# Low parts of streamed weights in a two-layer hybrid backbone: subtraction on VectorE, or negation and an adding transfer

## Chip, cores and metric

The kernel runs on one core of one Trainium2 chip. The metric is the device time of one execution in microseconds (us), lower is better. The engines are called PE (TensorE; PEld is its weight load), DVE (VectorE), ACT (ScalarE), POOL (GpSimd) and SP (SyncE, which issues most transfers).

## The reference

Two layers of a backbone over 256 latent tokens and 256 context tokens of width 1024, in float32. The large products with weights are what matters here:

```python
u = rms_norm(h, norm1_g[l]) * (1.0 + sc1) + sh1
a_x, a_g, b_q, b_f, b_i, b_o, c_qkv, m_g = split_projection(u @ w_in[l])
...
h = h + gt1 * merge_branches(ya, yb, yc, m_g, w_branch[l], w_out[l])
h = h + gt2 * sq_relu_ffn(rms_norm(h, norm2_g[l]) * (1.0 + sc2) + sh2, ffn_w1[l], ffn_w2[l])
```

Between them stand three mixers (a gated linear recurrence in chunks, a neighbourhood attention, a bidirectional RG-LRU). Layer 0 computes both token streams (512 columns), the second half of layer 1 only the latent stream (256 columns).

## The kernel before

All large weights stand in HBM as 296 pieces of 128 x 1024 float32 (512 KB), 148 for each layer, in the order of use. A product in float32 accuracy is made of three products in fp32r: with weight = hi + lo and activation = xhi + xlo, it adds hi·xhi, hi·xlo and lo·xhi. So each piece needs two tiles: `whi`, the rounded weight, and `wlo`, what rounding left.

`arriving` (L209) has SP load a piece into a `raw` tile (3 buffers). `weights` (L214) takes a `wlo` and a `whi` tile (4 buffers each) and calls `split` (L224): ACT casts `raw` to `whi` (L226), and DVE subtracts, `wlo = raw - whi` (L227). `mm3` (L233) then issues for each of 8 blocks of 128 rows the three products (L240, L241, L242), 24 matmuls for a piece; `mm3_pairs` (L246, products L253 to L255) does two pieces at a time, and `tok` (L1013, products L1027 to L1029) and `down_pieces` have groups that use four pieces at once.

The main loop (the end of `hybrid_kernel`) works piece by piece. `fetch(n)` calls `weights` until n pieces are ready; before a piece's products are issued three more are fetched (one more ahead of a group of four). With four buffers, the `wlo` and `whi` tiles that the piece three places ahead is to use are those that the piece just ended leaves. Between the runs of products `lanes.tick()` issues steps of the mixers' chains, on all engines. A scheduler at build time sets the order on each engine from this program.

The first four pieces (`tok` of the first head) come with a `raw` tile of their own from `start()`, and one of them is subtracted on POOL. POOL else has little: scaling of `gf`, the rotary tables `ctab` (`rope_tables`, L318), and 15 transfers: the attention's bias tables (`bias`, L960) and the LRU's weights (`gw`, L968). A transfer into a buffer waits in its queue until that buffer is free, and what stands behind it in the same queue waits too. SP's queue has the `raw` pieces and, from the second third of layer 0 on, 72 transfers of 512 KB for the modulation (`arow`, L343) and 8 of `araw`.

Of the kernel before, what the change touches and what calls it, by code (L numbers as in the profile page):

```python
# [10 lines left out]
F32 = mybir.dt.float32  # L11
# [5 lines left out]
ALU = mybir.AluOpType  # L17
# [9 lines left out]
NPIECE = 148  # L27
# [29 lines left out]
def merge_order(l):  # L57
    # some gates first, while the mixers' chains end
    count = {}
    for part in MERGE[l].split():  # L60
        bi = int(part[0])
        for what in part[1:]:
            i = count.get((bi, what), 0)
            count[bi, what] = i + 1
            yield bi, BRANCH_ORDER[bi], {"g": "gate", "p": "proj"}[what], i
# [35 lines left out]
class Piece:  # L101
    """Products with streamed weights: body(weights) yields after each run of products."""
# [5 lines left out]
class Lanes:  # L108
    """Chains of dependent steps that are issued between the runs of products.

    A step yields the time that the vector engine needs for what it issued, and how many runs more the chain waits."""
# [43 lines left out]
def hybrid_kernel(  # L155
# [58 lines left out]
    def weights(l, key, raw=None, eng=nc.vector):  # L214
        cols = {"tok": 4 * P, "proj": 2 * P}.get(key[0], P)
        raw = arriving(l, key) if raw is None else raw
        lo = wpool.tile([P, 1024], F32R, tag="wlo", name="wlo", bufs=4)
        hi = wpool.tile([P, 1024], F32R, tag="whi", name="whi", bufs=4)
        split(hi, lo, raw, eng=eng)
        v = lambda t: t.rearrange("p (k c) -> p k c", c=cols)  # L220
        return v(hi), v(lo)

    def split(hi, lo, src, scale=None, eng=nc.vector):
        # hi <- rounded part of scale * src, lo <- the rest  # L224
        if scale is None:
            nc.scalar.copy(hi, src)  # L226
            eng.tensor_tensor(out=lo, in0=src, in1=hi.bitcast(F32), op=ALU.subtract)  # L227
        else:
            nc.scalar.mul(hi, src, scale)
            nc.vector.scalar_tensor_tensor(  # L230
                out=lo, in0=src, scalar=scale, in1=hi.bitcast(F32), op0=ALU.mult, op1=ALU.subtract
            )
# [13 lines left out]
    def mm3_pairs(dsts, ws, x, nk, c0, c1):  # L246
        # two pieces at a time, so that x may still be arriving
        for i in range(0, len(dsts), 2):
            for k in range(nk):
                xhi, xlo = (t[:, c0:c1] for t in x(k))  # L250
                for p_, (whi, wlo) in zip(dsts[i:i + 2], ws[i:i + 2]):
                    d = p_[:, c0:c1]
                    nc.tensor.matmul(d, lhsT=whi[:, k, :], rhs=xhi, start=(k == 0), stop=False)  # L253
                    nc.tensor.matmul(d, lhsT=whi[:, k, :], rhs=xlo, start=False, stop=False)
                    nc.tensor.matmul(d, lhsT=wlo[:, k, :], rhs=xhi, start=False, stop=(k == nk - 1))  # L255
                if k % 2:
                    yield
# [5 lines left out]
    def layer_scalars():  # L263
# [13 lines left out]
        for l in range(DEPTH):  # L277
            # f = lb + (1 - lb) * (1 + tanh) / 2 as offset and slope
            lb = cpool.tile([P, 2, 2, 4], F32, name=f"lb{l}")
            if l == 0:  # L280
                nc.vector.tensor_copy(cum, e[:, :, 0, :])
            else:
                nc.vector.tensor_add(cum, cum, e[:, :, l, :])
            nc.vector.tensor_sub(lb[:, 0], cum, e[:, :, 0, :])
            nc.vector.tensor_scalar(out=lb[:, 1], in0=lb[:, 0], scalar1=-0.5, scalar2=0.5, op0=ALU.mult, op1=ALU.add)
            nc.vector.tensor_scalar(out=lb[:, 0], in0=lb[:, 0], scalar1=0.5, scalar2=0.5, op0=ALU.mult, op1=ALU.add)
            lbs.append(lb)
# [31 lines left out]
    def rope_tables(l):  # L319
        # ctab[:, cos|sin, tile, k|q, head, :], with the norm's gains and the scores' scale  # L320
        for sc in range(2):
            for i, qk in enumerate((1, 0)):
                g = gf[l][:, 2 * sc + qk, :]
                for hd in range(2):
                    for tt in range(2):
                        nc.gpsimd.tensor_tensor(out=ctab[:, sc, tt, i, hd, :], in0=cst[:, sc, tt, :], in1=g, op=ALU.mult)

# [1 line left out]
    mod = [cpool.tile([P, 3, 2, 16], F32, name=f"mod{l}") for l in range(DEPTH)]  # L329

    def modulation_rows():
        # most sections, a row for each feature: the vector engine has time while the tensor engine is busy
# [34 lines left out]
    def last_modulation():  # L367
        # the last section: four groups of columns in four parts of the array
# [55 lines left out]
    def column_sums(parts, n, tag="A"):  # L424
        # sums over the features, one column for each 128 tokens
        p_ = psum(tag, "nss")
        for c in range(n):
            for i, t in enumerate(parts):
                nc.tensor.matmul(
                    p_[:, c:c + 1], lhsT=t[:, c * P:(c + 1) * P], rhs=ones, start=(i == 0), stop=(i == len(parts) - 1)  # L430
                )
        return p_
# [5 lines left out]
    def spread(r, n, tag="A"):  # L438
        # a row of n * 128 columns in every partition
# [14 lines left out]
    def modulated(u, r, a, b, k, s):  # L454
        # u = h * r * a + b in high and low parts
# [29 lines left out]
    def small_rstd(ss, n, temps):  # L485
        # 1 / sqrt(ss / n + eps) for a few columns: a first guess from the exponent, two steps
# [6 lines left out]
        # with x = v * r * r: r * (15 - 10 x + 3 x^2) / 8, but for the factor 3 / 8, then r * (3 - x) / 2 with that factor  # L493
# [14 lines left out]
    def first_half():  # L508
        # the latent stream's norm, before its products are issued
# [5 lines left out]
    def hgrn(l, j, TF, Q, vtok, sog, ys):  # L515
# [4 lines left out]
        # products over blocks, states of the context stream  # L520
# [9 lines left out]
        # within blocks of 64 tokens, the blocks of a tile side by side  # L530
# [7 lines left out]
        def place(b, src, shift):  # L538
            # blocks in the upper (b = 0) or the lower half of the partitions
# [13 lines left out]
        def mixed(t, hh, c0, n):  # L553
            # [first halves of slot 0 | second halves of slot 1] of the 2*hh blocks in columns c0..c0+n
# [17 lines left out]
        # A^T[s, t] of both directions, level by level  # L572
        Tt = TF[:]
        width = T2
        for lev in range(8):
# [11 lines left out]
            # widen the products to blocks of 2*hh  # L587
# [30 lines left out]
        # final states of the context stream  # L618
# [18 lines left out]
        # outputs, token-major  # L637
# [34 lines left out]
    def attention(l, j, qk, vtok, bias, ys):  # L672
        Tq = T2 if l == 0 else TL
        misc = two_k("misc")
        # normalised keys and queries, token-major: [k | q] of two heads for each 128 tokens
# [23 lines left out]
        # rotary embedding of the latent tokens  # L699
# [48 lines left out]
        def softmax(qt, sc):  # L748
            # both heads at once
# [55 lines left out]
        def applied(qt):  # L805
            # both heads at once, in two parts of the array
# [87 lines left out]
    def fin_query(Tq, Q, p_):  # L894
        # twice the silu
# [5 lines left out]
    def fin_outgate(l, Tq, sog, p_):  # L901
        # the gain over four times (1 + tanh)
# [17 lines left out]
    def fin_gelu(Tq, ge, p_):  # L920
        # twice the tanh GeLU
# [12 lines left out]
    def mixer_pieces(l):  # L934
        T = T2 if l == 0 else TL
        heads = []
        for j in range(4):
# [9 lines left out]
            def opened(nm, m=m, j=j):  # L947
                # tiles of a chain, when its first piece begins
# [9 lines left out]
                if nm == "tok":  # L958
                    m.bias = four_k("bias", (4, TL))
                    (nc.gpsimd if l or j else nc.sync).dma_start(out=m.bias, in_=biasd[l, j])  # L960
                    # [v of both mixers | k and q], two blocks of tokens each
# [4 lines left out]
                if nm in ("ax", "ag") and not hasattr(m, "gw"):  # L966
                    m.gw = two_k("gw").rearrange("p (a b) -> p a b", b=P)
                    nc.gpsimd.dma_start(out=m.gw, in_=lruw[l, j])  # L968
# [21 lines left out]
            def group(ws, m=m, opened=opened, closed=closed):  # L990
                # the first products, while the modulation arrives
# [70 lines left out]
    def merge_pieces(l):  # L1062
# [7 lines left out]
        def gate_tile(bi, d):  # L1070
            # several gates in a tile
# [78 lines left out]
    def down_pieces(l, kind, sub, x, section, T, finished, after, pre=None):  # L1150
        # pieces d = 0..7 into the residual; with after, the last four by streams, so that a norm can start early
# [119 lines left out]
    def start():  # L1271
# [51 lines left out]
        def busy(n):  # L1323
            # keeps the tensor engine's clock up while the first data arrive
# [30 lines left out]
        def arrive():  # L1355
            # what the products of the first chunk need
# [11 lines left out]
        def later():  # L1368
            # what the products of the first chunks don't need
# [11 lines left out]
        def ahead(k, n):  # L1381
            # within the products of chunk k, what those of chunk k + 2 need
# [24 lines left out]
    # weights run ahead of the pieces that use them  # L1407
# [154 lines left out]
```

## Time and profile before

| what | us |
|---|---|
| two timed runs | 1528.32 and 1531.29 |
| their median | 1529.8 |
| span of the profiled execution, first to last instruction | 1526.3 |

The profile is of one execution. Its span leaves out what lies around the first and the last instruction; the median of the timed runs is 3.5 us above it, and that is taken as what lies around.

### The profile page before, as it was taken

The numbers are of one execution on the slowest core, as the hardware profiler recorded it, in microseconds if no ns is written. First come the engines' busy times: TensorE is split into PE (matmuls) and PEld (weight loads), VectorE is DVE, ScalarE is ACT, GpSimd is POOL, SyncE is SP. The second block draws the span as 40 slices with busy tenths as digits, with TensorE's granted clock in tenths as the row PEclk, the third lists the DMA queues.
The fourth block names the chain that finished last, engine by engine and source line by source line (L and its number), as shares of the span: only waits on it lengthen the run. The fifth ranks groups of instructions, "written<-read, shape, count | busy, mean of one in ns | idle before, by whom it ended". The sixth has DMA issues, their size and how long they took to land.

```text
span 1526.3 us, 24145 instructions
## 1 busy us (share of the span) xinstructions
PE 1513.7 (99%) x9554; PEld 1300.8 (85%) x9554; DVE 1115.9 (73%) x2118; ACT 735.0 (48%) x1229; POOL 26.4 (2%) x57
## 2 busy tenths in 40 slices
PE   9999999999999999999999999999999999999999
PEld 4778788878888889888888889888888899999999
DVE  6776768586478898988685856778787856776664
ACT  3457575666333333532322323475766854454442
POOL 0200000020000000000000000000000000000000
PEclk9999999999999999999999999999999999999999
DMA  9413122221273562445463532313313345755553
GB/s 368 146 53 104 56 90 70 70 77 62 91 250 136 187 240 70 171 174 206 139 220 127 204 126 82 133 63 126 104 70 105 109 167 182 274 167 184 186 183 125
DMA packets 61793, 217.36 MB, mean 142 GB/s; under 512 B 7792, under 2 KB 9456, under 8 KB 61680
## 3 DMA queue, kind: packets, MB, share of 16 engines
q1 hardware_dynamic: 59328, 209.88, 39.5%
q0 software_dynamic: 1648, 5.77, 1.2%
q8 instruction: 75, 1.23, 0.3%
q14 instruction: 38, 0.31, 0.1%
q10 hardware_dynamic: 704, 0.17, 0.1%
HBM read 214.74 MB, written 1.05 MB: 141 GB/s over the span
## 4 chain that ended last, share of the span: by engine, by line
PE 96%; DVE 2%; ACT 1%; issue 1%; DMA 0%; SPq 0%; DVEq 0%
PE pd L240 7%; PE pd L242 7%; PE pd L241 7%; PE pf L242 5%; PE pf L240 5%; PE pf L241 5%; PE pg L240 5%; PE pg L241 4%; PE pg L242 4%; PE ptok L1027 3%; PE ptok L1029 3%; PE ptok L1028 3%; PE lv L547 2%; PE pp L241 2%; PE pp L240 2%; PE pp L242 2%
## 5 line engine op out<-in xcount | busy, mean ns | idle before, releaser
L226 ACT CAST whi<-raw 128x1024 fp32r<-128x1024 f32 x296 | 310.3, 1050 | 477.0 <-PE pd L241 157.2
L227 DVE TENSOR_TENSOR wlo<-raw,whi 128x1024 fp32r<-128x1024 f32 x295 | 360.3, 1223 | 151.2 <-ACT whi L226 149.4
L242 PE MATMUL pd<-hhi,wlo 128*128 128x256 f32 (+1 forms) x544 | 177.8, 327 | 0.0
L240 PE MATMUL pd<-hhi,whi 128*128 128x256 f32 (+1 forms) x544 | 177.8, 327 | 0.0
L241 PE MATMUL pd<-hlo,whi 128*128 128x256 f32 (+1 forms) x544 | 177.7, 327 | 0.0
L354 DVE CUSTOM_DVE_ANT_0 junk<-arow,crow 128x1024 bf16<-128x1024 f32 x144 | 173.3, 1219 | 2.2 <-DMA arow<-in_adaw 2.0
L241 PE MATMUL pf<-xlo,whi 128*128 128x256 f32 (+1 forms) x464 | 155.0, 334 | 0.0
L242 PE MATMUL pf<-xhi,wlo 128*128 128x256 f32 (+1 forms) x464 | 155.0, 334 | 0.0
L240 PE MATMUL pf<-xhi,whi 128*128 128x256 f32 (+1 forms) x464 | 155.0, 334 | 0.0
L240 PE MATMUL pg<-xhi,whi 128*128 128x512 f32 (+1 forms) x384 | 131.5, 342 | 0.0
L241 PE MATMUL pg<-xlo,whi 128*128 128x512 f32 (+1 forms) x384 | 129.2, 336 | 0.0
L242 PE MATMUL pg<-xhi,wlo 128*128 128x512 f32 (+1 forms) x384 | 129.2, 336 | 0.0
L1145 DVE SCALAR_TENSOR_TENSOR h<-pd,mod,h 128x256 f32<-128x256 f32 x120 | 54.9, 480 | 81.2 <-PE pd L242 79.2
L241 PEld LDWEIGHTS pd<-hlo,whi 128*128 128x128 f32 x544 | 103.5, 190 | 8.8
L240 PEld LDWEIGHTS pd<-hhi,whi 128*128 128x128 f32 x544 | 103.5, 190 | 8.8
L242 PEld LDWEIGHTS pd<-hhi,wlo 128*128 128x128 f32 x544 | 103.5, 190 | 8.6
L241 PEld LDWEIGHTS pf<-xlo,whi 128*128 128x128 f32 x464 | 88.1, 190 | 8.8
L242 PEld LDWEIGHTS pf<-xhi,wlo 128*128 128x128 f32 x464 | 88.1, 190 | 8.7
L240 PEld LDWEIGHTS pf<-xhi,whi 128*128 128x128 f32 x464 | 88.0, 190 | 8.7
L1027 PE MATMUL ptok<-whi,xhi 128*128 128x512 f32 (+1 forms) x224 | 87.4, 395 | 1.1 <-DVE h L1145 1.1
L1029 PE MATMUL ptok<-wlo,xhi 128*128 128x512 f32 (+1 forms) x224 | 84.4, 377 | 0.0
L1028 PE MATMUL ptok<-whi,xlo 128*128 128x512 f32 (+1 forms) x224 | 84.2, 376 | 0.2 <-DVE xlo L463 0.2
(329 smaller groups left out, 3240.0 us busy)
## 6 DMA issues: line engine op xcount, KB each, us to landing
raw<-in_wpack SPq DMA_DIRECT2D x296, 512.0 KB, 3.5
arow<-in_adaw SPq DMA_DIRECT2D x72, 512.0 KB, 4.7
a<-in_ada0w SPq DMA_DIRECT2D x16, 512.0 KB, 10.4
araw<-in_lastw SPq DMA_DIRECT2D x8, 512.0 KB, 6.3
bias<-in_biasd POOLq DMA_DIRECT2D x7, 512.0 KB, 4.3
h<-in_xT SPq DMA_DIRECT2D x4, 512.0 KB, 5.5
gw<-in_lruw POOLq DMA_DIRECT2D x8, 256.0 KB, 2.9
out<-h SPq DMA_DIRECT2D x8, 128.0 KB, 2.0
```

What stands on the lines that cost most here:

```text
L226: nc.scalar.copy(hi, src)
L227: eng.tensor_tensor(out=lo, in0=src, in1=hi.bitcast(F32), op=ALU.subtract)
L240: nc.tensor.matmul(d, lhsT=whi[:, k, :], rhs=xhi, start=(k == 0), stop=False)
L241: nc.tensor.matmul(d, lhsT=whi[:, k, :], rhs=xlo, start=False, stop=False)
L242: nc.tensor.matmul(d, lhsT=wlo[:, k, :], rhs=xhi, start=False, stop=(k == nk - 1))
L354: nc.vector.tensor_tensor_reduce(out=junk, in0=raw, in1=crow[s], scale=1.0, scalar=0.0, op0=ALU.mult, op1=ALU.add, accum_out=section_of(l, ...
L547: nc.tensor.matmul(dst, lhsT=lhs(b), rhs=rhs(b), start=True, stop=True)
L1027: nc.tensor.matmul(dst, lhsT=xhi[:, k, tsl], rhs=whi[:, kk, :], start=(k == 0), stop=False)
L1028: nc.tensor.matmul(dst, lhsT=xlo[:, k, tsl], rhs=whi[:, kk, :], start=False, stop=False)
L1029: nc.tensor.matmul(dst, lhsT=xhi[:, k, tsl], rhs=wlo[:, kk, :], start=False, stop=(k == KD - 1))
L1145: nc.vector.scalar_tensor_tensor(out=h[:, d, sl], in0=p_[:, sl], scalar=mods(l, section, s)[:, d:d + 1], in1=h[:, d, sl], op0=ALU.mult, op ...
```

## The change

Except for the first four pieces, `wlo` is no longer subtracted. ACT makes `whi` from `raw` as before. DVE writes `wlo = -whi`, with one input. POOL then issues a transfer from HBM that reads the raw piece a second time and adds it to what stands in `wlo`. DVE's step no longer reads `raw`. The `bias` and `gw` transfers, which stood on POOL's queue, go to SP's.

```diff
     def weights(l, key, raw=None, eng=nc.vector):
         cols = {"tok": 4 * P, "proj": 2 * P}.get(key[0], P)
-        raw = arriving(l, key) if raw is None else raw
         lo = wpool.tile([P, 1024], F32R, tag="wlo", name="wlo", bufs=4)
         hi = wpool.tile([P, 1024], F32R, tag="whi", name="whi", bufs=4)
-        split(hi, lo, raw, eng=eng)
+        if raw is not None:
+            split(hi, lo, raw, eng=eng)
+        else:
+
+            nc.scalar.copy(hi, arriving(l, key))
+            nc.vector.tensor_scalar_mul(lo, hi.bitcast(F32), -1.0)
+            nc.gpsimd.dma_start(out=lo, in_=wpack[l * NPIECE + PIECE[key]], accum_op=ALU.add)
...
-                    (nc.gpsimd if l or j else nc.sync).dma_start(out=m.bias, in_=biasd[l, j])
+                    nc.sync.dma_start(out=m.bias, in_=biasd[l, j])
...
-                    nc.gpsimd.dma_start(out=m.gw, in_=lruw[l, j])
+                    nc.sync.dma_start(out=m.gw, in_=lruw[l, j])
```

On POOL the program before has, from the start of layer 0 on, this order (`gf` and `ctab` are the gains and the rotary tables, `msk` the masks of the recurrence, `gw` and `bias` the transfers named above; the numbers count buffers):

```order
L1375 TENSOR_SCALAR gf1_74<-gf1_74 128x64 x2
L326 TENSOR_TENSOR ctab_75<-cst_72,gf0_73 128x64 x8
L1379 CAST msk_76<-mskf_397 128x384
L968 DMA gw_808<-in_lruw 128x512
L960 DMA bias_1063<-in_biasd 128x1024
L968 DMA gw_1564<-in_lruw 128x512
L960 DMA bias_1814<-in_biasd 128x1024
L968 DMA gw_2329<-in_lruw 128x512
L960 DMA bias_2569<-in_biasd 128x1024
L326 TENSOR_TENSOR ctab_75<-cst_72,gf1_74 128x64 x16
L968 DMA gw_3094<-in_lruw 128x512
```

The changed program has there, and from there to its end:

```order
L1380 TENSOR_SCALAR gf_74<-gf_74 128x64 x2
L331 TENSOR_TENSOR ctab<-cst,gf_73 128x64 x8
L1384 CAST msk<-mskf 128x384
L224 DMA wlo<-in_wpack 128x1024 x36
L331 TENSOR_TENSOR ctab<-cst,gf_74 128x64 x16
L224 DMA wlo<-in_wpack 128x1024 x256
```

The 15 transfers are gone and 292 adding ones stand in their place, with the second set of tables between the 36th and the 37th.

On SP the program before has, from the last loads of the setup on (`raw` are the weight pieces, `mskf` the masks, `arow` the modulation's rows):

```order
L1376 DMA idh<-in_consts 128x64
L1378 DMA mskf<-in_masks 128x384
L211 DMA raw<-in_wpack 128x1024 x2
L960 DMA bias<-in_biasd 128x1024
L211 DMA raw<-in_wpack 128x1024 x53
```

The changed program has there:

```order
L211 DMA raw<-in_wpack 128x1024 x2
L965 DMA bias<-in_biasd 128x1024
L211 DMA raw<-in_wpack 128x1024 x8
L973 DMA gw<-in_lruw 128x512
L211 DMA raw<-in_wpack 128x1024 x2
L965 DMA bias<-in_biasd 128x1024
L211 DMA raw<-in_wpack 128x1024 x7
L973 DMA gw<-in_lruw 128x512
```

The transfers of `gw` and `bias` now stand between those of the pieces; the later ones stand in layer 1 in the same way.

## Rows read from the trace of the kernel before

**Rows 1.** Page, parts 1 and 2: busy us of each engine; TensorE's granted clock in 40 slices.
```profile
PE 1513.7 (99%) x9554; PEld 1300.8 (85%) x9554; DVE 1115.9 (73%) x2118; ACT 735.0 (48%) x1229; POOL 26.4 (2%) x57
...
PEclk9999999999999999999999999999999999999999
```

**Rows 2.** Page, part 4: the chain that ended last, by engine.
```profile
PE 96%; DVE 2%; ACT 1%; issue 1%; DMA 0%; SPq 0%; DVEq 0%
```

**Rows 3.** Windows: stretch, length, busy us (instructions) by engine, PEclk, DMA share, GB/s.
```profile
550.00:690.00 140.00, 138.38 (x795) 122.06 (x794) 122.78 (x223) 56.84 (x90) 0.00 (x0) 1.00 0.46 165
690.00:880.00 190.00, 190.00 (x840) 157.34 (x839) 145.43 (x229) 55.32 (x68) 0.00 (x0) 1.00 0.51 177
1188.00:1245.00 57.00, 57.00 (x482) 53.49 (x481) 40.46 (x84) 39.33 (x71) 0.00 (x0) 1.00 0.39 132
1245.00:1305.00 60.00, 60.00 (x502) 60.00 (x502) 42.45 (x69) 29.68 (x49) 0.00 (x0) 1.00 0.54 183
1305.00:1350.00 45.00, 43.55 (x391) 41.05 (x391) 33.50 (x70) 22.02 (x37) 0.00 (x0) 1.00 0.64 232
1350.00:1500.00 150.00, 150.00 (x1253) 150.00 (x1252) 97.35 (x140) 72.58 (x114) 0.00 (x0) 1.00 0.57 187
```

**Rows 4.** Timeline, layer 1's MLP: start, us, instruction [idle before it <- releaser].
```profile
1399.04 1.05 ACT L226 CAST whi<-raw 128x1024 fp32r<-128x1024 f32 x1 [1.79 <-PE pd L241]
...
1400.12 1.23 DVE L227 TENSOR_TENSOR wlo<-raw,whi 128x1024 fp32r<-128x1024 f32 x1 [0.47 <-ACT whi L226]
...
1407.84 0.28 PE L242 MATMUL pf<-xhi,wlo 128*128 128x256 f32 x1
```

**Rows 5.** Windows, only instructions on raw: DVE, ACT, POOL busy us (count), PEclk, DMA.
```profile
550.00:690.00 140.00, 30.47 (x25) 26.26 (x25) 0.00 (x0) 1.00 0.46 165
690.00:880.00 190.00, 42.87 (x35) 36.87 (x35) 0.00 (x0) 1.00 0.51 177
1188.00:1245.00 57.00, 17.03 (x14) 15.18 (x15) 0.00 (x0) 1.00 0.39 132
1245.00:1305.00 60.00, 25.71 (x21) 21.52 (x22) 0.00 (x0) 1.00 0.54 183
1305.00:1350.00 45.00, 14.92 (x13) 13.30 (x13) 0.00 (x0) 1.00 0.64 232
1350.00:1500.00 150.00, 64.68 (x53) 54.55 (x53) 0.00 (x0) 1.00 0.57 187
```

**Rows 6.** Groups by form, DVE: operation, shapes, count | busy us, mean ns | idle before.
```profile
L227 DVE TENSOR_TENSOR wlo<-raw,whi 128x1024 fp32r<-128x1024 f32 x295 | 360.3, 1223 | 151.2 <-ACT whi L226 149.4
L560 DVE COPY km<-KK 128x512 f32<-128x512 f32 x24 | 10.6, 440 | 1.9 <-PE lv L547 1.5 <-PE tp L793 0.3
L560 DVE COPY km<-KK 128x256 f32<-128x256 f32 x24 | 7.0, 293 | 0.6 <-PE tp L793 0.5
```

**Rows 7.** Tile bias: POOL's transfers of 512 KB, ns min/median/max; and time to landing.
```profile
L960 POOL DMA_DIRECT2D bias<-in_biasd x7: 536/536/542, 45.3 to 1097.6; - x7
...
DMA to landing us min/median/max: 3.6/5.3/7.5
```

**Rows 8.** DMA queues from 0 to 38 us: GB/s in 40 equal slices.
```profile
GB/s 0 6 183 356 343 350 393 379 376 423 384 302 418 414 405 410 414 427 418 418 423 418 414 440 397 410 414 414 435 418 418 414 427 414 427 377 373 336 344 230
```

**Rows 9.** Timeline, a `wlo` of a group's end and its first use: two of seven places.
```profile
604.52 1.22 DVE L227 TENSOR_TENSOR wlo<-raw,whi 128x1024 fp32r<-128x1024 f32 x1
...
605.94 0.40 PE L255 MATMUL pf<-xhi,wlo 128*128 128x256 f32 x2
...
1151.27 1.22 DVE L227 TENSOR_TENSOR wlo<-raw,whi 128x1024 fp32r<-128x1024 f32 x1
...
1156.81 0.40 PE L242 MATMUL pff<-xhi,wlo 128*128 128x512 f32 x1
```

**Rows 10.** Timeline of SP and of POOL as layer 1 nears: transfers.
```profile
880.01 0.33 SPq L211 DMA_DIRECT2D raw<-in_wpack  x1
...
881.77 0.54 POOL L960 DMA_DIRECT2D bias<-in_biasd  x1 [564.48 <-DVE mod L354]
```

## The prediction

> **What bounds the kernel now.** I read the page's busy times first, then the chain that ended last, then windows by stage, then the timeline of one piece, and last the transfers. PE is busy 1513.7 us, 99% of the span [rows 1], and 96% of the chain is PE [rows 2]; its granted clock is full all along [rows 1]. So an engine beside PE can save nothing but PE's idle time, 1526.3 - 1513.7 = 12.6 us. DVE, which the change relieves, is at 73% [rows 1] and stands for 2% of the chain [rows 2].
>
> The windows show that the stages differ in what lies behind PE [rows 3]. From 1245 us on (layer 1's merge and MLP, 256 columns) PE runs 1253 matmuls in 150 us; at 24 to a piece that is 52 pieces, one each 2.87 us, with the DMA engines at 0.57. From 690 to 880 us (layer 0's MLP, 512 columns) 840 matmuls take 190 us, 5.43 us a piece, with a DMA share of 0.51. The same weights are thus consumed almost twice as fast at the end.
>
> The timeline of one piece shows the slack [rows 4]. ACT starts a cast at 1399.04 when PE lets go of the buffer (1.79 us of idle before it, ended by PE), DVE has the low part ready at 1400.12 + 1.23 = 1401.35, and PE first reads it three pieces later, at 1407.84. So 6.5 us are free there.
>
> **The change, part by part.** *DVE.* 292 subtractions of 1223 ns go and 292 negations come, an operation with one input that no row has in this size. The nearest are copies: 293 ns for 256 columns and 440 ns for 512 [rows 6], which is 147 ns for 256 more, so 440 + 2 x 147 = 734 ns for 1024. From below I bound it by the 440 ns of half the size, from above by the subtraction's 1223; I take 0.73, as it continues a row of the nearest kind. DVE loses 292 x (1.22 - 0.73) = 143 us of work. What lies on the path is at most the 12.6 us above, and I take 0: PE does not wait for DVE in the long stages, whose windows are full.
>
> *The moved transfers.* `gw` and `bias` go from POOL's queue to SP's, where one that waits would hold up the pieces behind it. In the trace only one buffer came free late against its place on SP: at 881.77 us, while SP issued the next piece at 880.01 [rows 10]. A slip of 1.8 us stands before three loaded `raw` buffers; 0. POOL's tables now stand between two adding transfers, in layer 0, where the slack is larger than in rows 4; 0.
>
> *The adding transfers, as work of the DMA engines.* This is the term that decides. No row shows one. Each must bring 512 KB from HBM, fetch the 512 KB that stand in `wlo`, and write 512 KB. The nearest row is a plain transfer when the engines are saturated: 410 to 427 GB/s for most of the first 38 us [rows 8], so 524 KB / 420 GB/s = 1.25 us. Call the DMA engines' time for one adding transfer A. From below it is 1.25 us (the fetch and the addition are free, as if it were a plain one); less than a plain one, or a gain, I exclude, as the piece is still loaded once more. From above I take 4 us, some three plain ones: two reads, and a write that does not overlap them. I take two reads at the saturated rate, A = 2.5, since two sources go in for each result.
>
> A stage lasts at least as long as its DMA engines have work: share times length [rows 3] plus A for each piece, counted by ACT's casts [rows 5].
>
> - 690 to 880: 0.51 x 190 + 35 x 2.5 = 184 of 190 us, hidden; 550 to 690: 64 + 25 x 2.5 = 127 of 140, hidden.
> - 1188 to 1245: 22.2 + 15 x 2.5 = 59.7, +2.7.
> - 1245 to 1305: 32.4 + 22 x 2.5 = 87.4, +27.4.
> - 1305 to 1350: 28.8 + 13 x 2.5 = 61.3, +16.3.
> - 1350 to 1500: 85.5 + 53 x 2.5 = 218, +68.
>
> Together +114 us. Ahead of 550 us the pieces come more slowly and nothing is added.
>
> Here a rule of the Trainium skill can be weighed. What the rows have is only the plain rate [rows 8]. "Collectives: The Full Stack", in the section on the bandwidth ceiling, says of reductions done by the DMA engines that the addition itself is free and that the cost is the two source reads in the same ring, which halves the rate (measured there as a ratio of 1.93). By that rule A is 1.93 x 1.25 = 2.4 us (an estimate with that page's ratio) and the sum of the four stages +104. No row here shows it.
>
> *The adding transfers, as a longer chain.* After ACT's cast the old chain had 1.22 us; the new one has 0.73 on DVE, POOL's issue, and the landing. POOL's plain transfers of this size landed 3.6 to 7.5 us after issue, median 5.3 [rows 7]; with 1.25 for the second read I take 6.5. The chain becomes 0.73 + 6.5 - 1.22 = 6.0 us longer. In layer 0's long stretches and in rows 4 (6.5 us) that is covered. It is not covered where a group of four pieces ends and the next buffers come free late: seven places, of which the first leaves 605.94 - 605.74 = 0.2 us and the last 1156.81 - 1152.49 = 4.3 us [rows 9]; over the seven the mean is 3.0. So 7 x (6.0 - 3.0) = +21 us. What is queued behind POOL's wait for a negation is only further adding transfers; what is queued behind PE's wait is everything.
>
> A second rule speaks against the change: "SBUF — State Buffer", under who interferes with whom, says that a `tensor_scalar` in a two-port mode locks GpSimd out of the port by which it writes its descriptors. POOL's issue took 536 ns [rows 7], so each issue could start at most one negation later; by the rule the chain would be up to 0.73 us longer, 7 x 0.73 = 5 us in the sum above, and no row here has the two together.
>
> **The sum.** 1526.3 + 114 + 21 = 1661 us of span, and with the 3.5 us by which the median lies above the span, 1665 us. With the two reads at the tail's own mean (85.5 / 53 = 1.6 us a piece, rows 3 and 5; A = 3.1) the stages give 2 + 15 + 12 + 41 + 24 + 100 = +194, with 21 some 1745; with A = 2 they give 16 + 10 + 41 = +67 and 1618. This is the likeliest case's own range.
>
> **The rivals.**
>
> 1. *The addition rides along.* A = 1.25: 1245 to 1305 needs 32.4 + 27.5 = 59.9 of 60 us, 1350 to 1500 needs 85.5 + 66.3 = 152 of 150. The stages give +2, the chains with the plain landing of 5.3 us are 4.8 longer and give 7 x 1.8 = +13: 1545 us, no change that shows. For it speaks that the engines are half idle in every long window [rows 3]; against it, that a sum has two sources. It decides up to A = 1.4, where the stages cost 3 + 2 + 10 = 15.
> 2. *The adding pass is slow*, in the engines or in POOL's issue. A = 4: 24 + 47 + 25 + 60 + 36 + 148 = +340 over the six stages, and some +30 for the chains: 1900 us. For it speaks only that no row has such a transfer; against it, that POOL issues a plain one in 0.54 us [rows 7], and has 2.87 for each.
> 3. *PE gains from a lighter DVE.* At most 12.6 us [rows 1]: 1517 us, within what can't be told apart. Against it: PE's full windows [rows 3].
>
> **How the numbers follow.** A measurement of this kernel can tell about 2%, some 30 us, from no change. The forecast (A from 1.6 to 3.3) has 0.51, rival 1 0.23, rival 2 0.24, rival 3 0.02. Faster by over 2% would need more than PE's idle time: 0.02, kept for what I did not see. Rival 1 lies within 2%, less a little for longer landings: same 0.22. The rest is slower, 0.76. The range goes from 1540, just under rival 1, to 1900, rival 2's value, beyond which a slower adding pass has about one chance in eight.
>
> **What would show it.** Right: in the windows after 1245 us the DMA share is above 0.9, a piece takes 3.5 to 4.2 us where it took 2.87, and PE waits at L242 for `wlo` from the transfer; up to 550 us nothing moved. The adding transfer's queue shows twice a plain packet's time. Wrong: PE stays full in the last stage (rival 1), or the layer 0 windows grow too (rival 2); or SP's queue waits for a `bias` or `gw` buffer and PE for `raw`. It would also be wrong if PE's granted clock fell when it waits at each piece, since the matmuls are taken at their present length.

## The result and the profile after

The changed kernel takes 1674.1 us (median of two runs, 1673.14 and 1675.06) where the kernel before takes 1529.8: ratio 1.0945, 95% interval 1.0925 to 1.0965. It is slower by 9.4%; 1665 was predicted, in a range of 1540 to 1900. The span of the profiled execution grew from 1526.3 to 1672.9 us, by 146.6.

Parts 1 to 3 of the page of the kernel after: busy time by engine, TensorE's granted clock and the DMA engines in 40 slices, and the two queues that carry the weights (packets, MB, share of 16 engines; q0 holds POOL's transfers, q1 SP's).

```profile
PE 1561.2 (93%) x9554; PEld 1323.5 (79%) x9554; DVE 972.3 (58%) x2118; ACT 737.7 (44%) x1229; POOL 273.7 (16%) x334
...
PEclk9999999999999999999999999999999998899999
DMA  9838383757999957999999949559589999899998
...
q0 software_dynamic: 42048, 153.11, 49.3%
q1 hardware_dynamic: 61488, 215.65, 35.5%
```

DVE lost 143.6 us of work against [rows 1], and the kernel became slower by about as much; that the two agree is chance (the run without the second transfer, below). PE is no longer full: it idles for 1672.9 - 1561.2 = 111.7 us, against 12.6 before. The queues say what is full in its place: q0 carries the 292 adding transfers and holds the 16 engines for 49.3% of the span; q1, with 1.4 times the bytes, holds them for 35.5%.

Part 4, the chain that ended last, was 96% PE [rows 2]. Now the adding transfer is its largest single line (the shares that are listed add up to 44% of the span):

```profile
PE 16%; DMA 14%; issue 9%; ACT 2%; POOL 2%; DVE 1%; POOLq 0%; ACTq 0%
DMA wlo<-in_wpack 12%; POOL wlo L224 2%; DMA raw<-in_wpack 1%; PE pd L247 1%; PE pd L245 1%; PE pd L246 1%; PE pg L247 1%; PE pg L245 1%; PE pg L246 1%; PE ptok L1032 1%; PE pff L247 1%; PE ptok L1034 1%; PE lv L552 1%; PE ptok L1033 0%; PE sc L751 0%
```

The windows show in which stages the loss stands (columns as in [rows 3]). First layer 0's MLP, then two stretches of layer 1's merge and MLP, then the whole run cut in two where layer 1's merge begins:

```profile
690.00:880.00 190.00, 190.00 (x840) 157.34 (x839) 125.61 (x223) 57.90 (x74) 30.41 (x36) 1.00 1.00 270
...
1400.00:1550.00 150.00, 122.42 (x943) 114.22 (x944) 57.30 (x126) 58.23 (x95) 30.84 (x35) 0.95 1.01 264
1550.00:1670.00 120.00, 99.75 (x766) 93.26 (x765) 38.31 (x71) 35.36 (x46) 25.03 (x29) 1.00 1.02 260
...
18.00:1231.00 1213.00, 1180.36 (x6656) 973.65 (x6657) 785.36 (x1675) 559.50 (x944) 178.67 (x224) 0.99 0.80 206
1231.00:1672.00 441.00, 365.52 (x2812) 342.35 (x2811) 173.31 (x374) 170.72 (x272) 92.50 (x106) 0.97 1.01 261
```

and the same cut in the kernel before:

```profile
18.00:1188.00 1170.00, 1165.14 (x6658) 966.09 (x6658) 878.00 (x1675) 558.88 (x944) 23.86 (x52) 1.00 0.37 130
1188.00:1526.00 338.00, 333.51 (x2810) 327.29 (x2808) 224.21 (x374) 168.68 (x272) 0.00 (x0) 1.00 0.52 177
```

From 690 to 880 us layer 0's MLP lost nothing: PE is busy for all of the 190 us, although the DMA share rose from 0.51 [rows 3] to 1.00. Up to layer 1's merge the kernel lost 1213 - 1170 = 43 us: 28 of PE's idle time (32.6 against 4.9) and 15 of longer matmuls. From there it lost 441 - 338 = 103 us, 71 of idle time (75.5 against 4.5) and 32 of longer matmuls. A finer place comes from PE's matmuls counted by piece in both traces (24 for a piece, 48 for the 12 of layer 0 that are done stream by stream): below, the delay "at piece n" is how much later the last product of that piece begins than in the kernel before.

One piece of the tail, from the timeline of the kernel after: start, us, instruction [idle before it <- releaser]. The cast, the negation and the issue belong to one piece; the last line is that piece's first low product.

```profile
1506.91 1.04 ACT L222 CAST whi<-raw 128x1024 fp32r<-128x1024 f32 x1 [2.72 <-PE pd L246]
...
1507.99 0.69 DVE L223 TENSOR_SCALAR wlo<-whi 128x1024 fp32r<-128x1024 f32 x1 [0.47 <-ACT whi L222]
...
1509.21 0.86 POOL L224 DMA_DIRECT2D wlo<-in_wpack  x1 [2.90 <-DVE wlo L223]
...
1519.33 0.39 PE L247 MATMUL pf<-xhi,wlo 128*128 128x256 f32 x1 [0.68 <-DMA wlo<-in_wpack]
```

The cast to the low part was 2.3 us long in [rows 4]; here 12.4 us pass from the cast's start to the first use, 10.1 of them behind POOL's issue. POOL issues again every 3.8 us (1505.45, 1509.21, 1513.01): that is the step of a piece now, where it was 2.87. What the DMA engines do meanwhile is in the view of the transfers, 1450 to 1600 us (queues as above; then the issues, with the median us to landing):

```profile
q0 software_dynamic: 5656, 20.60, 68.9%
q1 hardware_dynamic: 5615, 20.46, 36.3%
...
wlo<-in_wpack POOLq DMA_DIRECT2D x40, 512.0 KB, 10.1
raw<-in_wpack SPq DMA_DIRECT2D x40, 512.0 KB, 9.4
```

Almost the same bytes stand in both queues. Per piece of 0.524 MB, q0 takes 0.689 x 150 / 39.3 = 2.63 us of all engines, q1 0.363 x 150 / 39.0 = 1.40. So an adding transfer costs 1.9 times a plain one, and the two together are 4.0 us a piece, at a summed share of 105%: 3.8 us.

The groups of the changed steps (columns as in [rows 6]), and from the view of the tile `wlo` the landing over the whole run:

```profile
L224 POOL DMA_DIRECT2D wlo<-in_wpack x292 | 256.7, 882 | 1353.8 <-DVE wlo L223 897.6
L223 DVE TENSOR_SCALAR wlo<-whi 128x1024 fp32r<-128x1024 f32 x292 | 202.0, 693 | 271.8 <-ACT whi L222 270.1
```

```profile
DMA to landing us min/median/max: 5.2/8.9/14.4
```

The median landing of the plain `raw` transfers rose with the load as well, from 3.5 to 7.7 us, and that of `arow` from 4.7 to 9.4.

### The profile page after: what moved, and what is told of

Its sections match the earlier page's. It is cut to its first block, busy times and chain, and to the rows that moved or that the text cites. A ratio compares the mean times of both kernels' runs of the same rounds, so it can differ in the third digit from the quotient of the medians.

```text
span 1672.9 us, 24755 instructions
## 1 busy us (share of the span) xinstructions
PE 1561.2 (93%) x9554; PEld 1323.5 (79%) x9554; DVE 972.3 (58%) x2118; ACT 737.7 (44%) x1229; POOL 273.7 (16%) x334
## 3 DMA queue, kind: packets, MB, share of 16 engines
q0 software_dynamic: 42048, 153.11, 49.3%
q1 hardware_dynamic: 61488, 215.65, 35.5%
## 5 line engine op out<-in xcount | busy, mean ns | idle before, releaser
L222 ACT CAST whi<-raw 128x1024 fp32r<-128x1024 f32 x292 | 306.1, 1049 | 582.7 <-PE pd L246 176.5
L224 POOL DMA_DIRECT2D wlo<-in_wpack x292 | 256.7, 882 | 1353.8 <-DVE wlo L223 897.6
L223 DVE TENSOR_SCALAR wlo<-whi 128x1024 fp32r<-128x1024 f32 x292 | 202.0, 693 | 271.8 <-ACT whi L222 270.1
L247 PE MATMUL pd<-hhi,wlo 128*128 128x256 f32 (+1 forms) x544 | 181.0, 333 | 19.7 <-DMA wlo<-in_wpack 19.6
L359 DVE CUSTOM_DVE_ANT_0 junk<-arow,crow 128x1024 bf16<-128x1024 f32 x144 | 173.9, 1220 | 27.4 <-DMA arow<-in_adaw 27.1
L247 PE MATMUL pf<-xhi,wlo 128*128 128x256 f32 (+1 forms) x464 | 159.4, 344 | 26.2 <-DMA wlo<-in_wpack 26.2
L247 PEld LDWEIGHTS pg<-xhi,wlo 128*128 128x128 f32 x384 | 74.2, 193 | 19.9 <-DMA wlo<-in_wpack 12.0
## 6 DMA issues: line engine op xcount, KB each, us to landing
a<-in_ada0w SPq DMA_DIRECT2D x16, 512.0 KB, 10.4
araw<-in_lastw SPq DMA_DIRECT2D x8, 512.0 KB, 12.4
```

Source lines behind the costliest of these rows:

```text
L222: nc.scalar.copy(hi, arriving(l, key))
L223: nc.vector.tensor_scalar_mul(lo, hi.bitcast(F32), -1.0)
L224: nc.gpsimd.dma_start(out=lo, in_=wpack[l * NPIECE + PIECE[key]], accum_op=ALU.add)
L359: nc.vector.tensor_tensor_reduce(out=junk, in0=raw, in1=crow[s], scale=1.0, scalar=0.0, op0=ALU.mult, op1=ALU.add, accum_out=section_of(l, ...
```

## The experiments

Every edit shown is one of the kernel after, except where said; every ratio is to the kernel before, measured on the same chip. That kernel had medians of 1526.21 us beside the first four runs, 1527.64 beside the next four and 1526.74 beside the last two.

**No second transfer.**

```diff
             nc.vector.tensor_scalar_mul(lo, hi.bitcast(F32), -1.0)
-            nc.gpsimd.dma_start(out=lo, in_=wpack[l * NPIECE + PIECE[key]], accum_op=ALU.add)
```

> The adding transfer is left out, so wlo stays the negated high part and the raw piece is not added. All theories: no wait of PE for a low part is left. If a lighter VectorE is worth anything, this shows it: at best 12.6 us less than before (1517 us), by my account nothing, 1522 to 1532.

1527.53 us, ratio 1.0005 (0.9995 to 1.0015). The whole loss hangs on the transfer, and DVE's 147 us less of work (969.3 against 1115.9 busy) are worth nothing.

**The same transfer without the addition.**

```diff
-            nc.gpsimd.dma_start(out=lo, in_=wpack[l * NPIECE + PIECE[key]], accum_op=ALU.add)
+            nc.gpsimd.dma_start(out=lo, in_=wpack[l * NPIECE + PIECE[key]])
```

> The transfer into wlo only copies the raw piece, so the low part is the whole weight and the subtraction is left out; HBM bytes, POOL's issue, order and chain stay. Two-reads theory (the second source, read from the tile itself, is what fills the DMA engines): the packets of the software queue fall from 327 to about 159 ns, the last stage returns to 2.9 to 3.0 us a piece and the time to 1545 to 1575 us, the rest being stalls at the groups of four. HBM theory (reading each piece twice from HBM is what is too much): 1660 to 1680, still 3.8 us a piece. Chain theory (the four buffers and the longer way to a low part set the pace): above 1600.

1563.63 us, ratio 1.0245 (1.0215 to 1.0275). A window of layer 1's MLP in this kernel, and its queues from 1400 to 1500 us:

```profile
1400.00:1500.00 100.00, 100.00 (x830) 99.48 (x830) 45.43 (x88) 49.29 (x72) 17.95 (x34) 1.00 1.04 363
```

```profile
q0 software_dynamic: 4990, 18.16, 53.7%
q1 hardware_dynamic: 4952, 18.04, 50.0%
```

The same bytes come from HBM, the same negation and wait stand in the chain, with an issue that is 0.33 us shorter, and PE is full again: 363 GB/s go through where the adding kernel moved 264 over the MLP. So neither HBM nor the order of the steps sets the tail's 3.8 us; the addition does. Per piece q0 takes 0.537 x 100 / 34.6 = 1.55 us here. Its 4 KB packets take 174 ns in the median over the run, where 159 was expected, and 328 in the kernel after. What is left, 37 us over the kernel before, stands in steps at the groups of pieces (20.5 us at piece 188, 35.4 at the end).

The tile's view gives POOL's time for an issue (ns, min/median/max) in this kernel, and in the kernel after:

```profile
L224 POOL DMA_DIRECT2D wlo<-in_wpack x292: 527/527/857, 45.9 to 1549.0; - x146
```

```profile
L224 POOL DMA_DIRECT2D wlo<-in_wpack x292: 853/862/1425, 47.5 to 1661.1; - x146
```

The adding issue takes 335 ns more, with the same DVE instruction ahead of it.

**Half of each piece added, half subtracted.**

```diff
-            nc.scalar.copy(hi, arriving(l, key))
-            nc.vector.tensor_scalar_mul(lo, hi.bitcast(F32), -1.0)
-            nc.gpsimd.dma_start(out=lo, in_=wpack[l * NPIECE + PIECE[key]], accum_op=ALU.add)
+            raw = arriving(l, key)
+            nc.scalar.copy(hi, raw)
+            nc.vector.tensor_scalar_mul(lo[:, :512], hi[:, :512].bitcast(F32), -1.0)
+            nc.gpsimd.dma_start(out=lo[:, :512], in_=wpack[l * NPIECE + PIECE[key]][:, :512], accum_op=ALU.add)
+            nc.vector.tensor_tensor(out=lo[:, 512:], in0=raw[:, 512:], in1=hi[:, 512:].bitcast(F32), op=ALU.subtract)
```

> Half the columns of a piece go by negation and adding transfer, the other half by VectorE's subtraction; the result is complete. Two-reads theory: 1.4 us for raw and 1.3 for the half are 2.7 of 2.88 us, so the last stage returns to PE's pace of 2.9 to 3.0 us a piece and the time is 1545 to 1575. Chain theory: the way to the low part is as long as before but for 1.3 us of landing, so the pace goes from 3.8 to no better than 3.4 us, about 1630.

1566.76 us, ratio 1.0265 (1.0248 to 1.0282). From 1400 to 1500 us PE is busy for 98.73 us and the queues have 50.3% each, so half the addition just fits beside PE. Per piece of 0.262 MB q0 takes 0.503 x 100 / 33.5 = 1.50 us, where 1.3 was expected. POOL's issue is 862 ns as for the whole addition, so it is not what sets the tail's 3.8 us. The chains remain: the landing is 5.8 us in the median, the delay 15.3 us at piece 188 and 37.5 at the end.

**A fifth buffer.** Five `wlo` and `whi` tiles, with pieces fetched one further ahead; room for them comes from work buffers, `N4` 11 in place of 13.

```diff
-N2, N4 = 25, 13
+N2, N4 = 25, 11
...
-        lo = wpool.tile([P, 1024], F32R, tag="wlo", name="wlo", bufs=4)
-        hi = wpool.tile([P, 1024], F32R, tag="whi", name="whi", bufs=4)
+        lo = wpool.tile([P, 1024], F32R, tag="wlo", name="wlo", bufs=5)
+        hi = wpool.tile([P, 1024], F32R, tag="whi", name="whi", bufs=5)
...
-            fetch(max(1, 4 - len(ws)))
+            fetch(max(1, 5 - len(ws)))
```

> Five wlo and whi buffers and one piece more fetched ahead; two fewer of the 4 KB work buffers make the room. Two-reads theory: the last stage stays at 3.8 us a piece, some 100 us over before, and only the stalls at the groups (43 us up to layer 1's merge) shrink: 1635 to 1660. Chain theory: a fifth buffer takes the pace from 3.8 to 3.8 x 3 / 4 = 2.9 us and the time to about 1560.

1640.31 us, ratio 1.073 (1.0696 to 1.0764). The trace is of the shortest of four executions, 1630.39 us; where the other three lost their 9 to 11 us more is not known. In it the delay at piece 188 fell from 43.3 to 5.2 us, so there the loss was a chain that came too late. The tail hardly moved: 97 us are lost from there on, against 103. The chain of waits of this kernel inside the MLP, and its queues from 1400 to 1500 us:

```profile
1438.32 10.32 DMA raw<-in_wpack
...
1448.74 1.06 ACT whi L222
...
1449.82 10.27 DMA raw<-in_wpack
```

```profile
q0 software_dynamic: 3761, 13.68, 68.6%
q1 hardware_dynamic: 3754, 13.67, 36.5%
```

The adding transfer has left the chain and the plain one stands in it, with a landing of 10.3 us. The queues' shares are those of four buffers. The three `raw` buffers now step at (10.3 + 1.1) / 3 = 3.8 us; as that landing was 3.5 us before, it is the full engines that stretch it. An adding transfer's median landing from 1400 to 1500 us is 13.3 us here, where the kernel after has 10.1 in its tail. A longer lead only makes each transfer wait longer: the engines are the bound.

**The work buffers alone** (`N4` 11, four weight buffers), the control for the run above.

> The changed kernel with the two fewer 4 KB work buffers of the five-buffer kernel, and nothing else: the control for it. If these buffers don't matter, 1665 to 1685 as the changed kernel; if they are what changed the stalls at the groups, less than 1655 or more than 1700.

1678.52 us, ratio 1.099 (1.0956 to 1.1024): no gain lies in that edit. That it costs something is not shown, as the interval overlaps that of the kernel after (1.0925 to 1.0965).

**Adding in layer 0 alone**, subtraction in layer 1.

```diff
+        if raw is None and l > 0:
+            raw = arriving(l, key)
```

> Adding transfers in layer 0 alone; layer 1 subtracts on VectorE as before. Two-reads theory: the 5.4 us a piece of layer 0 hide the engines' 4 us, so only the stalls at the groups are left, some 27 us up to layer 1: 1548 to 1562. Chain theory in the form that every piece pays for its longer way: over 1590.

1555.66 us, ratio 1.0186 (1.0165 to 1.0206). The delay is 6.7 us at piece 40, 25.1 at piece 92 and 25.9 from the end of layer 0 on. Against the kernel after, 1674.1 - 1555.7 = 118 us are layer 1's.

**Five buffers with half of each piece added**, the two edits above together.

> Five wlo and whi buffers, and half of each piece's columns by adding transfer, half by subtraction. Two-reads theory: both terms go, the engines' (2.7 of 2.88 us a piece) and the groups': 1528 to 1545. If instead the half transfer's 37 us over before are the engines', they stay: about 1560.

1540.55 us, ratio 1.0082 (1.0067 to 1.0097). With the chain covered and the engines' load cut, what is left is 12.5 us of the span, nearly all of it behind piece 188: 10.4 come between pieces 223 and 236, where the groups stand that end layer 1's merge and begin its MLP.

**Five buffers with adding in layer 0 alone.**

> Five wlo and whi buffers, adding transfers in layer 0 alone. Two-reads theory: nothing is left to pay, 1525 to 1535; VectorE is lighter by some 75 us in layer 0 and that gains nothing. If a lighter VectorE is worth something after all, below 1520.

1533.65 us, ratio 1.0041 (1.0028 to 1.0055): 6 us are left, under the 2% of a verdict, though the interval excludes 1. No version with adding transfers beat the kernel before.

**Layer 0 alone, groups spared.** Four buffers. Beside layer 1, the pieces next to groups of four keep the subtraction: three behind each head's group, the last four of the merge and the first five of the MLP, 21 of 144.

```diff
+        late = key[0] in ("ff", "fb", "hq") or key[0] == "out" and key[1] > 3 or key[0] == "f1" and key[1:] < (0, 5)
+        if raw is None and (l > 0 or late):
+            raw = arriving(l, key)
```

> Four buffers, adding in layer 0 alone, and near its groups of four pieces (ff, fb, hq, out from the fifth on, f1 up to its fifth piece of the first quarter) the old subtraction. If layer 0's +26 us (against the kernel before, at equal pieces) come from the longer chain at the groups alone: 1526 to 1537 us. If they come from the load of the adding transfers wherever they stand: 1545 or more, near the 1556 of adding in all of layer 0. Below 1520 would say that a lighter DVE is worth something.

1533.9 us, ratio 1.0047 (1.0031 to 1.0063). Sparing 21 pieces took 1.4 points off the 1.9% that layer 0 costs, while the DMA share from 690 to 880 us stayed at 1.00. So in layer 0 it is where the adding transfers stand that costs, hardly how many there are; a run that spares 21 other pieces was not made.

**The moved transfers alone**: the kernel before, with `gw` and `bias` on SP's queue.

```diff
-                    (nc.gpsimd if l or j else nc.sync).dma_start(out=m.bias, in_=biasd[l, j])
+                    nc.sync.dma_start(out=m.bias, in_=biasd[l, j])
...
-                    nc.gpsimd.dma_start(out=m.gw, in_=lruw[l, j])
+                    nc.sync.dma_start(out=m.gw, in_=lruw[l, j])
```

> The kernel before with one part of the change alone: the gw and bias transfers go to SP's queue, every low part is still subtracted. My theory, that the moved transfers cost nothing beside pieces that are loaded ahead: 1525 to 1531 us, ratio 0.998 to 1.003, and the raw landing stays at the kernel before's. The rival, that part of the loss at the groups comes from gw and bias holding up the pieces behind them: 1540 or more, and PE waits for raw or whi near 45, 560 or 880 us.

1527.64 us, ratio 1.000 (0.9987 to 1.0012). They cost nothing.

## Why the prediction was right, step by step

*The bound.* That PE's idle time was all that a lighter engine could give held, and it gave none of it: without the transfer the kernel runs as before, at 693 ns for a negation (734 was taken).

*A, the DMA engines' time for an adding transfer.* Taken 2.5 us, measured 2.63 in the saturated tail. The rule of the Trainium skill that the prediction weighed ("Collectives: The Full Stack", the bandwidth ceiling: the addition is free, the second read is not, ratio 1.93) agrees with the 2.63 / 1.40 = 1.9 measured here. That it is the second read that takes this time, and not the addition, no run separates. Rival 1, the addition that rides along, falls by the run without the addition; rival 2, A = 4, falls by the same 2.63.

*The stages.* +114 was the sum, 103 the measured loss from layer 1's merge on. By the delays at the pieces that stood at the windows' edges before, the four terms 2.7, 27.4, 16.3 and 68 came out as 5.6, 19.7, 19.7 and 53.7, and 4.6 more came behind 1500 us, where the sum had nothing. The last term failed in its working: to the share of a half-loaded window, 85.5 us for 53 pieces or 1.61 each, I added A, 4.1 us a piece. A plain piece shrinks to 1.40 when the engines are full, and the two shares overlap by 5%, so a piece takes 3.81 us (pieces 256 to 277 in 80.0). Bytes would have given it, with an adding transfer as two reads: three reads of 0.524 MB at the 420 GB/s of [rows 8] are 3.75 us. The 53.7 also has a step of 7.1 us at a wait of 4.8 us (1440 to 1450) behind the MLP's first group; as the four pieces behind it lose only 0.5 us together, some 3 us of it are more than the steady loss of 0.93 a piece.

*The chains.* This term was mis-sized, 21 us for 43.3. The step that failed is "with 1.25 for the second read I take 6.5" and the count of seven places. The landing was 8.9 us in the median over the run. Part of this belongs to the adding transfer itself. From 100 to 300 us, where `raw` lands in 3.6 us as before (3.5), the median is 7.6; a plain transfer in its place takes 5.4. The issues in that window, first in the kernel after, then in the run without the addition:

```profile
raw<-in_wpack SPq DMA_DIRECT2D x24, 512.0 KB, 3.6
wlo<-in_wpack POOLq DMA_DIRECT2D x24, 512.0 KB, 7.6
...
raw<-in_wpack SPq DMA_DIRECT2D x25, 512.0 KB, 3.6
wlo<-in_wpack POOLq DMA_DIRECT2D x25, 512.0 KB, 5.4
```

The rest is load: when the adding transfers fill the engines they delay themselves (10.1 from 1450 to 1600 us) and every other transfer. The plain landing was also misread. The 5.3 of [rows 7] is the median of all eight `bias` transfers, one of which, at 7.5 us, is SP's. POOL's seven have 4.3, with which the term would have been some 14 us.

And the delay steps up at more places than seven: 4.3 us at piece 14, 4.4 at 35, 16.4 from piece 80 to 88 where two groups stand close together, 10.5 from 148 to 152, then 1.3 to 1.7 at each head of layer 1. So the sign "up to 550 us nothing moved" failed too: the delay there was 10.3 us. That the landing sets this term is borne out in the main: at piece 188 the delay is 43.3 us with the whole addition (landing 8.9), 15.3 with half of it (5.8) and 20.5 with a plain transfer (5.4). The last two stand the other way round than their landings, and no run shows why.

So one term was 11 us too large and the other 22 too small. The 3.5 us outside the span were too many as well: they set the span of one execution against the median of two, and in each execution on record 1.8 to 2.2 us lie outside. That 1665 came within 9 us of 1674 is in part luck.

The error of the chains lay in rival 1 as well, which was to end 15 us above the kernel before, too little to be told apart: the plain transfer ends 37 us above, slower by 2.4%.

*POOL's issue* was taken as a plain one, 0.54 us, and is 0.86. The other rule weighed, of the Trainium skill's "SBUF — State Buffer" (who interferes with whom), would have a negation hold up POOL's writing of descriptors. It does not explain the 0.86: the plain transfer behind the same negation takes 0.53.

*The clock* was named as what could make the prediction wrong, and in part it fell. After the longer waits PE ran for some microseconds at half the full clock. The timeline behind the MLP's first group in layer 0, and five windows: one behind a wait of 3.12 us that ended at 612.39 us, one behind the wait of that timeline, one in the steady tail, and the time from the middle of layer 1's merge on, cut in two:

```profile
643.09 0.40 PE L246 MATMUL pf<-xlo,whi 128*128 128x512 f32 x1
647.69 0.80 PE L247 MATMUL pf<-xhi,wlo 128*128 128x512 f32 x1 [4.21 <-DMA wlo<-in_wpack]
648.29 0.63 PE L245 MATMUL pf<-xhi,whi 128*128 128x512 f32 x1
648.72 0.63 PE L246 MATMUL pf<-xlo,whi 128*128 128x512 f32 x1
...
650.97 0.40 PE L246 MATMUL pf<-xlo,whi 128*128 128x512 f32 x1
651.20 0.39 PE L247 MATMUL pf<-xhi,wlo 128*128 128x512 f32 x1
```

```profile
613.00:619.80 6.80, 5.04 (x25) 4.75 (x24) 4.00 (x8) 0.42 (x1) 0.86 (x1) 0.50 0.54 139
...
647.20:650.60 3.40, 2.91 (x7) 2.33 (x8) 0.10 (x1) 0.62 (x1) 0.34 (x1) 0.50 1.06 278
1505.00:1520.00 15.00, 12.29 (x96) 11.48 (x95) 4.62 (x8) 4.18 (x4) 3.45 (x4) 1.00 1.05 275
...
1271.00:1461.00 190.00, 157.07 (x1188) 148.66 (x1188) 76.59 (x174) 70.64 (x121) 39.23 (x44) 0.92 1.01 268
1461.00:1670.00 209.00, 172.03 (x1318) 160.87 (x1318) 69.64 (x132) 70.35 (x100) 44.90 (x52) 1.00 1.03 267
```

After 4.21 us without work the products start 0.43 us apart in place of 0.23, which is the 1.2 GHz level: granted 0.50 in the second window. So a wait at a group costs itself and then slow matmuls; the 15 us of longer matmuls up to layer 1's merge stand beside a granted clock of 0.99 there. From layer 1's merge on, with 32 us of longer matmuls, the mean is 0.97: it is 0.92 from 1271 to 1461 us, which has the groups of the merge's end and the MLP's start, and 1.00 behind. In that tail, where PE waits 0.7 us for every piece, the first matmul after each wait still takes 0.39 us in place of 0.28. The share of the clock in the loss was read from these rows; no run held it apart from the waits.

## What to carry to other kernels

A transfer that adds into SBUF from HBM cost about as much here as two plain ones, and is priced so: before work is handed from an engine to it, add up the bytes in the stage with the least time per piece, those of the adding transfer twice, and divide by the rate that the trace shows when the DMA engines are full. Taking 147 us of work off an engine that stood for 2% of the chain gave nothing. An operation that becomes a transfer adds its own landing under the new load, not that of a plain transfer under the old one, wherever buffers come free late. A deeper buffer tells the two apart: it takes away what a late chain costs and leaves what throughput costs.

## What the runs showed of the hardware

An adding transfer of 512 KB holds the 16 DMA engines for 2.63 us where a plain one takes 1.40 in the same window, though HBM gives the same bytes for both. In the kernel after no adding transfer landed in less than 5.2 us, and in no run one of a whole piece in less than 5.1; the plain ones in their place (the run without the addition) took 3.7 at least and 5.4 in the median. POOL's time for an issue rises with the addition, from 527 to 862 ns, and is 862 ns for half the columns as well, so it does not go by the bytes. The half transfer has about as many packets as the whole (4815 for 33.5 pieces against 5656 for 39.3), so whether it goes by the transfer or by its packets is not shown.
